# Up projection of a two-layer encoder: all products with rounded weights of a half block ahead of those with remainders, and weight tiles without their offset

## The chip, the core and the metric

The kernel runs on one core of one Trainium2 chip. Its time is device microseconds (us) of one execution, as the median of several runs. Beside the time there is one profiled execution, in which every instruction of every engine has a start and a length.

## What is computed

Two encoder layers over 256 tokens of width 2048, all in float32. Each layer normalises, projects into two groups of attention heads, projects back, normalises again and ends in a gated feed-forward part with a depthwise convolution. The change touches the up projection of that last part, the product `h2 @ w_up[l]` of 256 tokens with 2048 x 11264 weights:

```python
h2 = rms_norm(x, ln2_g[l])
u = depthwise_conv(h2 @ w_up[l], conv_w[l], conv_b[l])
gate, up = u[..., :D_FF], u[..., D_FF:]          # D_FF = 5632
x = x + (jax.nn.silu(gate) * up) @ w_down[l]
```

## The kernel before

A float32 matrix product is made from products of shorter numbers (type float32r). Every operand is split into a rounded part and a remainder. For weights ScalarE writes the rounded part `whi` (line 112) and VectorE the remainder `wlo = raw - whi` (line 113). For tokens the tile `xs[k]` of 128 partitions x 2 x 256 holds the rounded part in slot 0 and the remainder in slot 1, for the k-th of the 16 groups of 128 input columns. Three of the four products of the parts are kept.

All weights come from memory once, in quanta of 128 x 2048 (`raw`, three buffers, issued by the sync engine's queue at line 741). Each quantum is used in two halves of 128 x 1024 (three for some of the down projection). `split_w` (line 751) makes `whi` and `wlo` of a half four halves ahead of its use; there are five buffers of each. A scheduler places the instructions of each engine, with priorities that the code gives; on TensorE the matmuls stand nearly as the code writes them.

The up projection is done in blocks of 128 gate columns and 128 up columns (j = 0 and 1). There are 44 blocks in a layer, 88 in all, each of two quanta, so of four halves; 352 halves in all. One half holds 4 of the 16 k for both j, so 8 weight tiles of 128 x 128. In `q_up` (line 524) the weights are the stationary operand and the tokens move. The helper `two` (line 411) makes two matmuls of a weight tile:

- the rounded weights with both slots of the tokens, 512 columns wide (called a hi product below),
- the remainder with slot 0 of the tokens, 256 columns wide (a lo product).

So one half is hi, lo, hi, lo, ... eight times. When a block's last half is done, `glu` (line 539) reads the sums, applies the convolution and the gate, and splits the result for the down projection.

Everywhere else in the kernel (input, output and down projection) tokens are stationary and 512 weight columns move. The attention of the second head group (`scores` at line 335 and `values` at line 386, through `thrice` at line 328) makes 256-wide float32r matmuls in direct succession.

Where operands lie matters to the change. The tiles of `raw`, `whi`, `wlo`, `mid` and `xs` lie one after the other in each partition's memory, and all their sizes (8192, 4352, 4352, 2048 and 2048 bytes) are whole multiples of 256 bytes, so their starts are equal modulo 256. A weight tile has 1024 + 64 columns of 4 bytes. The up projection uses columns 56 to 1079 of it (`UP_AT = 56`), so its weights start 224 bytes further than its tokens, modulo 256. All other quanta use columns 0 to 1023, in line with what they are multiplied with. "In line" below means: the next weights to be loaded start at the same place modulo 256 bytes as the operand that is moving.

Of the kernel before, what the change touches and what calls it, by code (L numbers as in the profile page):

```python
# [12 lines left out]
F32R = mybir.dt.float32r  # L13
# [5 lines left out]
P = 128  # L19
# [4 lines left out]
KD = D // P  # L24
# [24 lines left out]
SPLIT_AHEAD = 4  # L49
AHEAD_PRIO = 40  # L50
SHIFT = 48

UP_AT = 56
WARM = 14

SPARE = 3 * (("qT", 3),)
# [3 lines left out]
def encoder_kernel(  # L60
# [7 lines left out]
    wp = ctx.enter_context(tc.tile_pool(name="wp", bufs=2))  # L68
# [28 lines left out]
    def mm(ps, lhsT, rhs, start, stop):  # L97
        nc.tensor.matmul(ps, lhsT, rhs, start=start, stop=stop, skip_group_check=True)  # L98
# [10 lines left out]
    def split(hi, lo, src, scale=None):  # L109

        if scale is None:
            high = nc.scalar.activation(hi, src, AF.Copy)  # L112
            nc.vector.tensor_sub(lo, src, hi.bitcast(F32))  # L113
        else:
            high = nc.scalar.activation(hi, src, AF.Copy, scale=scale)  # L115
            nc.vector.scalar_tensor_tensor(lo, src, scale, hi.bitcast(F32),
                                           op0=ALU.mult, op1=ALU.subtract)
        return high
# [7 lines left out]
    xs = {}  # L126
# [281 lines left out]
    def at(q, f, *args, half=1):  # L408
        side.setdefault((q, half), []).append((f, args))

    def two(ps, w_h, w_l, mv, first, last):

        mm(ps, w_h, mv, first, False)
        mm(ps[:, 1], w_l, mv[:, 0], False, last)

    def three(ps, terms, hv, lv, first, last, apart=False):

# [109 lines left out]
    def q_up(l, f, u):  # L527
        def body(q, half, hi, lo):
            if u == 0 and half == 0:
                cur["up"] = psum.tile([P, 2, 2, T], F32, name="mm", bufs=2)  # L530
            ps = cur["up"]
            hv, lv = (w.rearrange("p (k j n) -> p k j n", k=4, j=2) for w in (hi, lo))
            for j in range(2):
                for kk in range(4):
                    k = 8 * u + 4 * half + kk
                    two(ps[:, j], hv[:, kk, j], lv[:, kk, j], xs[k], k == 0, k == KD - 1)
            if u == 1 and half == 1:
                glu(l, f, ps)
        return body

    def glu(l, f, ps):
        ux = halo[f % 2]
        r = T // GRID_W
        t = work.tile([P, 2, T], F32, name="prob", bufs=2)
        nc.scalar.activation(t, ps[:, :, 0], AF.Copy)  # L545
        nc.vector.tensor_add(t, t, ps[:, :, 1])  # L546
        nc.vector.tensor_mul(ux[:, :, r:r + T], t, st["r2"][:, None, :].to_broadcast([P, 2, T]))  # L547

        nc.gpsimd.tensor_copy(ux[:, :, 1:r], ux[:, :, T:T + r - 1])  # L549
        nc.gpsimd.tensor_copy(ux[:, :, T + r:T + 2 * r - 1], ux[:, :, r + 1:2 * r])  # L550
        y = work.tile([P, 2, T], F32, name="pT", bufs=4)
        for j in range(2):
            c = j * NF + f
            w0, w1, w2, b = (par["conv"][:, l, i, c:c + 1] for i in range(4))
            nc.scalar.activation(y[:, j, :], ux[:, j, r:r + T], AF.Identity, scale=w1, bias=b)  # L555
            for w, o in ((w0, 0), (w2, 2 * r)):
                nc.vector.scalar_tensor_tensor(y[:, j, :], ux[:, j, o:o + T], w, y[:, j, :],  # L557
                                               op0=ALU.mult, op1=ALU.add)
        nc.scalar.activation(t[:, 0, :], y[:, 0, :], AF.Silu)  # L559
        m = work.tile([P, T], F32, name="bias", bufs=2)  # L560
        nc.vector.tensor_mul(m, t[:, 0, :], y[:, 1, :])
        gs[f] = middle(l, f)
        split(gs[f][:, 0], gs[f][:, 1], m)
        ms[f] = m
        if f % 2 and f < NF - CHUNKS[-1] + PART:
            sums_mid(l, f // 2, ms.pop(f - 1), ms.pop(f))
# [132 lines left out]
    for l in range(L):  # L699
# [8 lines left out]
        for c, nf in enumerate(CHUNKS):  # L708
            up = lambda f: [(a["w_up"][l, f, u], q_up(l, f, u), "up") for u in range(2)]
# [23 lines left out]
    raw, hl, left, loads, highs = {}, {}, {}, {}, {}  # L733

    def load(q, parts=1):
        if q < len(quanta):
            raw[q] = wp.tile([P, 2048], F32, name="raw", bufs=3)
            left[q] = 3 if quanta[q][2] == "seven" else 2
            m = 2048 // parts
            for j in range(parts):  # L740
                loads[q] = nc.sync.dma_start(out=raw[q][:, j * m:(j + 1) * m], in_=quanta[q][0][:, j * m:(j + 1) * m])

    def split_seven(w, part, hi, lo):

        hv, lv = (t.rearrange("p (k n) -> p k n", k=2) for t in (hi, lo))
        if part == 1:
            nc.vector.tensor_sub(w[:, 1:3], w[:, 1:3], w[:, 2:4])
            nc.vector.tensor_add(w[:, 3], w[:, 3], w[:, 1])
            nc.vector.tensor_sub(w[:, 0], w[:, 3], w[:, 0])
        return split(hv, lv, (w[:, 1::2], w[:, 1:3], w[:, 0::3])[part])  # L750

    def split_w(s, parts=1):
        if s < len(steps):
            q, half = steps[s]
            kind = quanta[q][2]
            o = UP_AT if kind == "up" else 0
            hl[s] = tuple(wp.tile([P, 1024 + 64], F32R, name=t, bufs=SPLIT_AHEAD + 1)[:, o:o + 1024]
                          for t in ("whi", "wlo"))
            with tc.high_priority(offset=AHEAD_PRIO if s >= KD // 2 else 0):
                if kind == "seven":  # L760
                    highs[s] = split_seven(raw[q].rearrange("p (k n) -> p k n", k=4), half, *hl[s])
                else:
                    m = 1024 // parts
                    for j in range(parts):
                        highs[s] = split(*(t[:, j * m:(j + 1) * m] for t in hl[s]),
                                         raw[q][:, half * 1024 + j * m:half * 1024 + (j + 1) * m])
            left[q] -= 1
            if left[q] == 0:
                del raw[q]
                load(q + LOAD_AHEAD)  # L770
# [61 lines left out]
    ps = psum.tile([P, T], F32, name="pv", bufs=1)  # L832
# [3 lines left out]
    for i in range(SPLIT_AHEAD):  # L836
        first_x(i)
        split_w(i, 2 if i == 0 else 1)
# [14 lines left out]
    for s, (q, half) in enumerate(steps):  # L853
        if s + SPLIT_AHEAD < KD // 2:
            first_x(s + SPLIT_AHEAD)
        split_w(s + SPLIT_AHEAD)
        quanta[q][1](q, half, *hl.pop(s))
        for f, args in side.pop((q, half), []):
            f(*args)
# [101 lines left out]
```

## Time and profile before

| what | value |
|---|---|
| median of 3 runs | 2092.17 us (2092.07 to 2092.38) |
| the profiled execution | 2092.0 us, with a span of 2090.2 us from its first to its last instruction |
| TensorE matmuls (PE) busy | 2083.5 us, 100% of the span, 10816 instructions |
| VectorE (DVE) busy | 1720.5 us, 82% |
| ScalarE (ACT) busy | 1222.3 us, 58% |
| GpSimd (POOL) busy | 170.3 us, 8% |
| hi products of the up projection | 2816, mean 390 ns |
| lo products of the up projection | 2816, mean 282 ns |

The matmul's length runs from its start to its modelled end, and the next one starts well before that end; so 390 ns is not the time that a matmul takes from the engine. What it takes is the distance from its start to the start of the next one, called its step below. In the views, L98 is the helper `mm` that issues every matmul; matmuls are told apart by the tiles that they read and write. `PE` rows are matmuls, `PEld` rows the loads of their stationary operand.

### The profile page before, as it was taken

The page shows a single profiled execution, that of the slowest core. Times are in us where ns is not written, and L with a number is a line of the kernel's source. Part 1 is how long each engine was busy: PE and PEld are TensorE (multiplying, and loading weights), DVE is VectorE, ACT ScalarE, POOL GpSimd, SP SyncE. Part 2 cuts the span into 40 slices and gives each one's busy share as a digit, 9 for nine tenths or more (in the row PEclk, how much of TensorE's full clock was granted, in tenths as well). Part 3 has the DMA queues.
Part 4 walks back from the last instruction along what each step waited for, and adds up shares of the span by engine and source line. Part 5 has one row for each costly group of instructions (what it writes and reads, how often), then busy time and mean ns, then how long its engine had stood idle before and what let it go on. Part 6 is the DMA issues. An engine that isn't in the chain of part 4 may idle for free.

```text
span 2090.2 us, 29185 instructions
## 1 busy us (share of the span) xinstructions
PE 2083.5 (100%) x10816; PEld 1789.2 (86%) x10816; DVE 1720.5 (82%) x2604; ACT 1222.3 (58%) x1817; POOL 170.3 (8%) x237
## 2 busy tenths in 40 slices
PE   9999999999999999999999999999999999999999
PEld 8888888888888888888888888888888888888887
DVE  7786757898898988989757866678989989899896
ACT  7566556555555556556555665565556555555563
POOL 0011100100101001010000011001001010010100
PEclk9999999999999999999999999999999999999999
DMA  9544555556565564655655444555555655556554
GB/s 350 199 145 164 179 172 174 198 195 211 180 241 182 208 210 167 242 193 211 208 181 181 162 160 166 177 182 189 214 202 170 236 199 204 201 185 234 185 200 161
DMA packets 62144, 408.42 MB, mean 195 GB/s; under 512 B 7344, under 2 KB 9904, under 8 KB 13744
## 3 DMA queue, kind: packets, MB, share of 16 engines
q1 hardware_dynamic: 61280, 405.46, 56.2%
q8 instruction: 85, 1.39, 0.3%
q10 hardware_dynamic: 720, 1.08, 0.2%
q14 instruction: 59, 0.48, 0.1%
HBM read 404.42 MB, written 2.10 MB: 194 GB/s over the span
## 4 chain that ended last, share of the span: by engine, by line
PE 99%; DMA 0%; ACT 0%; DVE 0%; issue 0%
PE mm L98 90%; PE S L98 4%; PE pv L98 3%; PE tr L98 2%; PE tr L373 1%; PE tr L307 1%; PE S L149 1%; DMA head<-in_head 0%; ACT qtok L274 0%; ACT kT L315 0%; ACT xs L115 0%; DVE x L688 0%; ACT whi L112 0%
## 5 line engine op out<-in xcount | busy, mean ns | idle before, releaser
L112 ACT ACTIVATE whi<-raw 128x1024 fp32r<-128x1024 f32 (+1 forms) x797 | 830.9, 1057 | 689.9 <-PE mm L98 411.9
L113 DVE TENSOR_TENSOR wlo<-raw,whi 128x1024 fp32r<-128x1024 f32 (+1 forms) x797 | 963.9, 1220 | 270.3 <-ACT whi L112 231.8
L98 PE MATMUL mm<-xs,whi 128*128 128x512 f32 x2816 | 977.0, 390 | 0.0
L98 PE MATMUL mm<-xs,wlo 128*128 128x256 f32 x2816 | 794.1, 282 | 0.0
L98 PEld LDWEIGHTS mm<-xs,whi 128*128 128x128 f32 x2816 | 528.3, 188 | 110.5
L98 PEld LDWEIGHTS mm<-xs,wlo 128*128 128x128 f32 x2816 | 532.2, 189 | 1.1
L98 PE MATMUL mm<-whi,mid 128*128 128x512 f32 x1412 | 368.2, 391 | 0.0
L98 PEld LDWEIGHTS mm<-whi,mid 128*128 128x128 f32 x1412 | 263.0, 188 | 53.9
L98 PE MATMUL mm<-whi,xs 128*128 128x512 f32 x1152 | 294.2, 393 | 1.4 <-ACT qtok L274 1.3
L98 PEld LDWEIGHTS mm<-whi,xs 128*128 128x128 f32 x1152 | 213.1, 188 | 44.7 <-ACT qtok L274 1.8
L98 PE MATMUL mm<-wlo,mid 128*128 128x512 f32 x706 | 202.4, 392 | 0.0
L98 PE MATMUL mm<-wlo,xs 128*128 128x512 f32 x576 | 159.5, 393 | 0.0
L98 PEld LDWEIGHTS mm<-wlo,mid 128*128 128x128 f32 x706 | 132.1, 188 | 27.0
L557 DVE SCALAR_TENSOR_TENSOR pT<-halo,conv,pT 128x256 f32<-128x256 f32 x352 | 148.1, 478 | 0.9
L549 POOL COPY halo<-halo 128x6 f32<-128x6 f32 x88 | 39.6, 450 | 1232.6 <-DVE halo L547 1232.6
L98 PEld LDWEIGHTS mm<-wlo,xs 128*128 128x128 f32 x576 | 107.3, 188 | 21.6
L555 ACT ACTIVATE pT<-halo,conv 128x256 f32<-128x256 f32 x176 | 95.1, 587 | 5.8 <-DVE halo L547 5.7
L550 POOL COPY halo<-halo 128x6 f32<-128x6 f32 x88 | 77.1, 876 | 0.2 <-POOL halo L549 0.2
L547 DVE TENSOR_TENSOR halo<-prob,acc_b 128x512 f32<-128x512 f32 x88 | 60.6, 689 | 1.9
L546 DVE TENSOR_TENSOR prob<-prob,mm 128x512 f32<-128x512 f32 x88 | 59.8, 679 | 0.0
L545 ACT ACTIVATE prob<-mm 128x512 f32<-128x512 f32 x88 | 51.3, 583 | 7.1 <-PE mm L98 7.1
L559 ACT ACTIVATE prob<-pT 128x256 f32<-128x256 f32 x88 | 35.5, 404 | 30.0 <-DVE pT L557 30.0
(180 smaller groups left out, 1475.4 us busy)
## 6 DMA issues: line engine op xcount, KB each, us to landing
raw<-in_w_up SPq DMA_DIRECT2D x176, 1024.0 KB, 4.9
raw<-in_w_in SPq DMA_DIRECT2D x71, 1024.0 KB, 4.9
raw<-in_w_down SPq DMA_DIRECT2D x48, 1024.0 KB, 4.8
raw<-in_w_seven SPq DMA_DIRECT2D x40, 1024.0 KB, 4.9
raw<-in_w_out SPq DMA_DIRECT2D x32, 1024.0 KB, 4.9
raw<-in_w_plain SPq DMA_DIRECT2D x10, 1024.0 KB, 4.8
bias<-in_bias SPq DMA_DIRECT2D x16, 160.0 KB, 3.1
x<-in_x SPq DMA_DIRECT2D x4, 512.0 KB, 10.7
```

What stands on the lines that cost most here:

```text
L98: nc.tensor.matmul(ps, lhsT, rhs, start=start, stop=stop, skip_group_check=True)
L112: high = nc.scalar.activation(hi, src, AF.Copy)
L113: nc.vector.tensor_sub(lo, src, hi.bitcast(F32))
L149: nc.tensor.transpose(ps[:, j, tt * P:(tt + 1) * P], x[:, tt, (k + j) * P:(k + j + 1) * P], ident)
L545: nc.scalar.activation(t, ps[:, :, 0], AF.Copy)
L546: nc.vector.tensor_add(t, t, ps[:, :, 1])
L547: nc.vector.tensor_mul(ux[:, :, r:r + T], t, st["r2"][:, None, :].to_broadcast([P, 2, T]))
L549: nc.gpsimd.tensor_copy(ux[:, :, 1:r], ux[:, :, T:T + r - 1])
L550: nc.gpsimd.tensor_copy(ux[:, :, T + r:T + 2 * r - 1], ux[:, :, r + 1:2 * r])
L555: nc.scalar.activation(y[:, j, :], ux[:, j, r:r + T], AF.Identity, scale=w1, bias=b)
L557: nc.vector.scalar_tensor_tensor(y[:, j, :], ux[:, j, o:o + T], w, y[:, j, :], op0=ALU.mult, op1=ALU.add)
L559: nc.scalar.activation(t[:, 0, :], y[:, 0, :], AF.Silu)
```

## The change

The eight hi products of a half come first and then its eight lo products. The constant `UP_AT` and the 64 spare columns of the weight tiles are gone: every weight tile is 128 x 1024, and the up projection's weights start in line with its tokens.

```diff
-
-UP_AT = 56
 WARM = 14
@@
-    def two(ps, w_h, w_l, mv, first, last):
-
-        mm(ps, w_h, mv, first, False)
-        mm(ps[:, 1], w_l, mv[:, 0], False, last)
+    def two(terms):
+
+        for ps, w_h, w_l, mv, first, last in terms:
+            mm(ps, w_h, mv, first, False)
+        for ps, w_h, w_l, mv, first, last in terms:
+            mm(ps[:, 1], w_l, mv[:, 0], False, last)
@@
             hv, lv = (w.rearrange("p (k j n) -> p k j n", k=4, j=2) for w in (hi, lo))
-            for j in range(2):
-                for kk in range(4):
-                    k = 8 * u + 4 * half + kk
-                    two(ps[:, j], hv[:, kk, j], lv[:, kk, j], xs[k], k == 0, k == KD - 1)
+            two([(ps[:, j], hv[:, kk, j], lv[:, kk, j], xs[k], k == 0, k == KD - 1)
+                 for j in range(2) for kk, k in enumerate(range(8 * u + 4 * half, 8 * u + 4 * half + 4))])
@@
-            o = UP_AT if kind == "up" else 0
-            hl[s] = tuple(wp.tile([P, 1024 + 64], F32R, name=t, bufs=SPLIT_AHEAD + 1)[:, o:o + 1024]
-                          for t in ("whi", "wlo"))
+            hl[s] = tuple(wp.tile([P, 1024], F32R, name=t, bufs=SPLIT_AHEAD + 1) for t in ("whi", "wlo"))
```

On TensorE, the second half of a middle block stands like this before (`mm_5708` is the block's accumulator, `xs4_2892` to `xs7_2906` are the tokens of four k, `whi_5610` and `wlo_5611` the half's weights):

```order
L98 MATMUL mm_5708<-xs4_2892,whi_5610 128x512
L98 MATMUL mm_5708<-xs4_2892,wlo_5611 128x256
L98 MATMUL mm_5708<-xs5_2895,whi_5610 128x512
L98 MATMUL mm_5708<-xs5_2895,wlo_5611 128x256
L98 MATMUL mm_5708<-xs6_2903,whi_5610 128x512
L98 MATMUL mm_5708<-xs6_2903,wlo_5611 128x256
L98 MATMUL mm_5708<-xs7_2906,whi_5610 128x512
L98 MATMUL mm_5708<-xs7_2906,wlo_5611 128x256
```

and the same half, on TensorE, with the first two products of the half that follows, stands like this now (the helper is line 96 there):

```order
L96 MATMUL mm_5708<-xs6_2903,whi_5610 128x512
L96 MATMUL mm_5708<-xs7_2906,whi_5610 128x512
L96 MATMUL mm_5708<-xs4_2892,wlo_5611 128x256
L96 MATMUL mm_5708<-xs5_2895,wlo_5611 128x256
L96 MATMUL mm_5708<-xs6_2903,wlo_5611 128x256
L96 MATMUL mm_5708<-xs7_2906,wlo_5611 128x256
L96 MATMUL mm_5708<-xs4_2892,wlo_5611 128x256
L96 MATMUL mm_5708<-xs5_2895,wlo_5611 128x256
L96 MATMUL mm_5708<-xs6_2903,wlo_5611 128x256
L96 MATMUL mm_5708<-xs7_2906,wlo_5611 128x256
L96 MATMUL mm_5708<-xs8_2989,whi_5632 128x512
L96 MATMUL mm_5708<-xs9_2992,whi_5632 128x512
```

The matmuls are the same; runs of eight 512-wide and eight 256-wide ones have taken the place of the alternation, and a run of lo products is followed by the hi products of the next half.

On VectorE, around the end of a layer's first up block, the subtraction of the next weights (`wlo`) and the sum that empties the accumulator (`prob<-prob,mm`) stand like this before:

```order
L113 TENSOR_TENSOR wlo<-raw,whi 128x1024 x3
L546 TENSOR_TENSOR prob<-prob,mm 128x512
L547 TENSOR_TENSOR halo_110<-prob,acc_b 128x2x256
L113 TENSOR_TENSOR wlo<-raw,whi 128x1024
L557 SCALAR_TENSOR_TENSOR pT<-halo_110,conv,pT 128x256 x4
L113 TENSOR_TENSOR wlo<-raw,whi 128x1024
```

and like this now:

```order
L111 TENSOR_TENSOR wlo<-raw,whi 128x1024 x2
L544 TENSOR_TENSOR prob<-prob,mm 128x512
L111 TENSOR_TENSOR wlo<-raw,whi 128x1024
L545 TENSOR_TENSOR halo_110<-prob,acc_b 128x2x256
L111 TENSOR_TENSOR wlo<-raw,whi 128x1024
L555 SCALAR_TENSOR_TENSOR pT<-halo_110,conv,pT 128x256 x4
```

The same instructions stand there; single ones have changed places with a neighbour.

## Rows read from the trace of the kernel before

**Rows 1.** The page: span, busy engines, granted clock, chain that ended last.
```profile
span 2090.2 us, 29185 instructions
PE 2083.5 (100%) x10816; PEld 1789.2 (86%) x10816; DVE 1720.5 (82%) x2604; ACT 1222.3 (58%) x1817; POOL 170.3 (8%) x237
...
PEclk9999999999999999999999999999999999999999
...
PE 99%; DMA 0%; ACT 0%; DVE 0%; issue 0%
PE mm L98 90%; PE S L98 4%; PE pv L98 3%; PE tr L98 2%; PE tr L373 1%; PE tr L307 1%; PE S L149 1%; DMA head<-in_head 0%; ACT qtok L274 0%; ACT kT L315 0%; ACT xs L115 0%; DVE x L688 0%; ACT whi L112 0%
```

**Rows 2.** Waits, TensorE's and ScalarE's: us in total, times, longest us.
```profile
PE mm L98 <- ACT qtok L274: 1.3, 2, 0.7
PE pv L98 <- DVE halfpi L94: 1.1, 1, 1.1
...
ACT whi L112 <- PE mm L98: 411.9, 330, 3.9
```

**Rows 3.** The page's groups, up projection: xcount | busy us, mean ns | idle before.
```profile
L98 PE MATMUL mm<-xs,whi 128*128 128x512 f32 x2816 | 977.0, 390 | 0.0
L98 PE MATMUL mm<-xs,wlo 128*128 128x256 f32 x2816 | 794.1, 282 | 0.0
```

**Rows 4.** Timeline, up projection, TensorE: start us, length us.
```profile
899.45 0.39 PE L98 MATMUL mm<-xs,whi 128*128 128x512 f32 x1
899.67 0.28 PE L98 MATMUL mm<-xs,wlo 128*128 128x256 f32 x1
...
904.99 0.39 PE L98 MATMUL mm<-xs,whi 128*128 128x512 f32 x1
```

**Rows 5.** Timeline, down projection, TensorE: 28 matmuls from first to last row.
```profile
440.28 1.98 PE L98 MATMUL mm<-whi,mid 128*128 128x512 f32 x8
...
446.63 1.52 PE L98 MATMUL mm<-whi,mid 128*128 128x512 f32 x6
```

**Rows 6.** Groups of that stretch, 440.2 to 447.8 us.
```profile
L98 PE MATMUL mm<-whi,mid 128*128 128x512 f32 x18 | 4.7, 389 | 0.0
```

**Rows 7.** Timeline, TensorE, around six 256-wide score matmuls.
```profile
111.22 1.09 PE L98 MATMUL mm<-wlo,xs 128*128 128x512 f32 x4
112.14 0.28 PE L98 MATMUL S<-kTb,qT 128*128 128x256 f32 x1
...
112.86 2.00 PE L98 MATMUL mm<-whi,xs 128*128 128x512 f32 x8
114.70 0.62 PE L98 MATMUL mm<-wlo,xs 128*128 128x512 f32 x2
```

**Rows 8.** Groups, TensorE, 112.15 to 112.90 us (the six score matmuls).
```profile
L98 PE MATMUL S<-mid,qT 128*128 128x256 f32 x2 | 0.6, 283 | 0.0
L98 PE MATMUL S<-kTb,mid 128*128 128x256 f32 x2 | 0.6, 282 | 0.0
L98 PE MATMUL S<-kTb,qT 128*128 128x256 f32 x2 | 0.6, 280 | 0.0
```

**Rows 9.** Groups, TensorE, 112.90 to 114.60 us, then 1153.55 to 1155.5 us.
```profile
L98 PE MATMUL mm<-whi,xs 128*128 128x512 f32 x8 | 2.0, 392 | 0.0
...
L98 PE MATMUL mm<-whi,xs 128*128 128x512 f32 x7 | 1.8, 393 | 0.0
```

**Rows 10.** Timeline, TensorE, after 256-wide matmuls of the values.
```profile
115.84 2.02 PE L98 MATMUL mm<-whi,xs 128*128 128x512 f32 x8
117.69 0.62 PE L98 MATMUL mm<-wlo,xs 128*128 128x512 f32 x2
...
172.07 0.85 PE L98 MATMUL pv<-pT,v_b 128*128 128x256 f32 x6
172.76 1.99 PE L98 MATMUL mm<-whi,xs 128*128 128x512 f32 x8
174.59 0.62 PE L98 MATMUL mm<-wlo,xs 128*128 128x512 f32 x2
```

**Rows 11.** Timeline, TensorE, from the up to the down projection.
```profile
430.75 1.08 PE L98 MATMUL mm<-whi,mid 128*128 128x512 f32 x4
431.67 0.62 PE L98 MATMUL mm<-wlo,mid 128*128 128x512 f32 x2
```

## Prediction

> **What bounds the kernel now.** I read the profile's page first. TensorE is busy for 2083.5 of 2090.2 us, the chain that ended last is 99% TensorE, and the granted clock is at its upper level (2.4 GHz) in all forty slices [rows 1]. The waits come second: TensorE waits for named releasers for 1.3 + 1.1 us in all, and none of these waits is in the up projection, while ScalarE, which makes the rounded weights, waits for TensorE for 411.9 us to get a buffer back [rows 2]. So weights are ready ahead of need, and time can come or go only in the steps of the matmuls.
>
> Third, the groups and the timeline give the steps. The up projection has 2816 hi and 2816 lo products, of mean length 390 and 282 ns [rows 3]. From 899.45 to 904.99 us there are 16 pairs, 5.54 us, so 346 to 347 ns a pair; a hi step is close to 228 ns and a lo step close to 118 (899.67 to the next hi, 346.5 less 228) [rows 4]. A half of eight pairs is 8 x 346.6 = 2.773 us, and 352 halves are 976 us, 47% of the span.
>
> In the down projection, where 512-wide matmuls in line follow each other, 28 of them take 446.63 - 440.28 = 6.35 us: a step of 226.8 ns [rows 5], at a mean length of 389 ns [rows 6]. A hi product is 1 ns longer in length and 1 ns longer in its step than these. A matmul that is held up shows it in its length, nanosecond for nanosecond; that gives steps finer than the 10 ns of the timeline.
>
> **The change part by part.** It adds and removes no matmul, no load and no byte from memory. Three things move.
>
> *The order and the place of the weights* are one term, since they act on the same thing: how long each of the 16 matmuls of a half holds the engine. The trace of before shows what the new sequence is made of, in the attention phase: 512-wide matmuls in line, then six 256-wide score matmuls in line, then 512-wide ones in line [rows 7].
>
> - The lo run. Six 256-wide matmuls take 112.86 - 112.14 = 0.72 us, 120 ns each [rows 7]; their mean lengths, two each of 283, 282 and 280, give 281.7 ns [rows 8], against 282 of the lo products now. Eight such: no gain, no loss, within 1 ns each.
> - The hi run behind it. After the score matmuls the eight 512-wide ones take 114.70 - 112.86 = 1.84 us, not 8 x 226.8 = 1.81 [rows 7]: the first few are held up and the rest fall back to the steady step. Their mean length is 392 ns, and 393 for seven in the same place of the second layer [rows 9], against 390 of the hi products now. That is 2 to 3 ns each, 16 to 24 ns per half; I take 20.
>
> So what the change wins by putting hi products side by side (390 to 389 ns once steady) is less than what it pays at each passage from lo to hi. Before, the alternation had passages too, but their price is already in the 390 and 282. Sum for a half: 8 x 0 + 20 ns; for 352 halves 352 x 20 ns = 7.0 us more.
>
> By the starts alone the sum would be 1.84 + 8 x 0.12 = 2.80 us against 2.773, 27 ns a half or 9.5 us. These starts are rounded to 10 ns, so I stay with the lengths.
>
> Bounds of this term: the cheapest 256-wide run in the trace takes 172.76 - 172.07 = 0.69 us for six, 115 ns each, and the cheapest 512-wide run is the steady one; 8 x 115 + 8 x 226.8 = 2.734 us, 39 ns less than now, 14 us in all. The dearest 512-wide run is 117.69 - 115.84 = 1.85 us; with lo at 120 that is 2.81, 37 ns more, 13 us in all [rows 5, 7, 10]. The score matmuls are nearest in kind, because they alone are in line, as the lo products will be; the values are not.
>
> *The ends of the up projection.* It gives over to the down projection 16 times. Now the four matmuls behind it take 0.92 us where 4 x 226.8 is 0.907 [rows 11], some 10 ns extra; behind a run of lo products I expect the 30 ns (1.84 less 1.81) of rows 7. 16 x 20 ns = 0.3 us.
>
> *Waits.* `whi` is a single tile, needed at the first product of a half as before; `wlo` is now needed 1.8 us into the half instead of 0.2, which only relieves. `whi` is given back some 0.7 us sooner, behind the eighth hi product. VectorE's and ScalarE's instructions change places with neighbours, by a subtraction at a time; ScalarE's 411.9 us of waiting for TensorE [rows 2] is the cover. Cost 0. If that cover failed at every hand-over, the price would be a wait of the size seen, 0.7 us at most [rows 2], in 16 places: 11 us; nothing speaks for it.
>
> *Everything else* keeps its alignment: ten weight tiles shrink by 256 bytes each, so what lies behind them moves by 2560 bytes, a whole multiple of 256. Cost 0: the 18 matmuls of rows 6 take their weights from several of these buffers in turn, and their mean is the steady 389 ns [rows 6].
>
> The Trainium skill speaks against any effect. "TensorE: Matmul & The Clock Gate", Part 2, says that TensorE has two independent SBUF read ports, one for the streaming operand and one for the weight load, so that loading the next weights takes nothing from the running matmul. By that page alone neither address nor order would count and the sum would be 0. The trace disagrees in size: the same 512-wide form has 389 ns in one neighbourhood and 392 to 393 in another [rows 6, 9].
>
> Sum: 2092.0 us of the profiled execution (span 2090.2 and 1.8 around it) + 7.0 + 0.3 = 2099.3 us. That execution lies 0.2 us below the median, which is nothing here.
>
> **The rivals.**
>
> *No change.* The passage from lo to hi costs nothing inside the up projection, because tokens move there and weights are stationary, the other way round than behind the score matmuls. Then a half is 8 x 226.8 + 8 x 120 = 2.774 us, the 2.773 of now: 2092. For it: the alternation has a passage at every pair and still costs only 346.6, which is 226.8 + 120 to a nanosecond [rows 4, 5, 7]. Against: the hold-up comes behind scores and values alike [rows 7, 10]. This is also where that rule of the Trainium skill leads.
>
> *Faster.* The lo run, once by itself, settles in the cheaper state that the six value matmuls reach at 172.07, 115 ns a step, and the hi run behind it costs what it costs there, 174.59 - 172.76 = 1.83 us [rows 10]. A half is 0.92 + 1.83 = 2.75, 23 ns less: 8 us, 2084. It decides as soon as the lo step stays below 117. For it: eight are a longer run than six. Against: those value matmuls are not in line, and the six in line stay at 120.
>
> *Slower still.* The hi run pays what it pays at 115.84, 1.85 us, with lo at 120: 13 us, 2105. Against it: that passage, too, is behind operands out of line.
>
> *The change does not do what it says.* If the weight tiles landed out of line, the price would lie between these; their sizes leave little room.
>
> **How the numbers follow.** My forecast 0.58, no change 0.14, faster 0.15, slower still 0.11, waits or tiles out of place 0.02. About 0.2% (4.2 us) is what a measurement of this kernel tells from no change. Slower by more: 0.58 + 0.11 less a little for a forecast that comes out at half its size, 0.67. Within: 0.17. Faster: 0.16. The forecast's own range is 2096 to 2103 (hi runs at 392 to 393, starts rounded). The range that should hold reaches down through no change, to 2088, and up to 2105.5; it leaves out most of the faster case.
>
> **What would show it.** In the profile after, the group of hi products has a mean of 392 to 393 instead of 390, and lo stays at 281 to 283. In the timeline a half takes 2.79 to 2.80 us, eight hi 1.84 and eight lo 0.95 to 0.96, with the hold-up in the first five hi products. TensorE still waits for next to nothing. A hi mean of 389 or a lo mean below 279 would show the forecast wrong in its first term; new waits of TensorE for `whi` or `wlo` would show the third wrong; other lengths in the down projection the fourth.

## The result, and the profile after

The changed kernel takes 2098.76 us (median of 8 runs, 2098.64 to 2099.07) against 2092.14 us before (8 runs, 2091.98 to 2093.0). The ratio is 1.0031, with a 95% interval of 1.0021 to 1.0041: slower by 6.6 us. The forecast was 2099.3 us, in a range of 2088.0 to 2105.5.

The page of the kernel after gives the span, the busy engines and the two groups of the up projection, with their mean lengths in ns behind the comma. They answer to [rows 1] and [rows 3]:

```profile
span 2097.0 us, 29183 instructions
...
PE 2089.7 (100%) x10816; PEld 1788.5 (85%) x10816; DVE 1722.0 (82%) x2604; ACT 1223.9 (58%) x1817; POOL 108.4 (5%) x237
...
PEclk9999999999999999999999999999999999999999
...
L96 PE MATMUL mm<-xs,whi 128*128 128x512 f32 x2816 | 705.2, 392 | 0.0
...
L96 PE MATMUL mm<-xs,wlo 128*128 128x256 f32 x2816 | 393.5, 282 | 0.0
```

The span grew by 6.8 us, TensorE is still busy all of it at the upper clock, hi products grew from 390 to 392 ns in the mean, and lo products stayed at 282. (The busy time of the groups is a union in time; runs of one kind overlap themselves, so it can't be compared with that of an alternation. The mean can.)

TensorE's waits, in us in total, times, and the longest, answer to [rows 2]:

```profile
PE mm L96 <- ACT qtok L272: 1.3, 2, 0.7
PE pv L96 <- DVE halfpi L92: 1.1, 1, 1.1
PE mm L96 <- ACT whi L110: 0.5, 1, 0.5
```

One wait of 0.5 us is new. It lies ahead of the first product of the input projection, which starts at the same time as before, so it costs nothing (the first row is the kernel before, the second the kernel after; start and length in us):

```profile
6.74 1.26 PE L98 MATMUL mm<-whi,xs 128*128 128x512 f32 x3
6.75 1.25 PE L96 MATMUL mm<-whi,xs 128*128 128x512 f32 x3 [0.46 <-ACT whi L110]
```

So nearly all of the 6.8 us is in the steps of matmuls, where [rows 4] are to be compared with this timeline of the kernel after (start, length of the merged run, count at the end):

```profile
899.04 2.00 PE L96 MATMUL mm<-xs,whi 128*128 128x512 f32 x8
900.89 1.11 PE L96 MATMUL mm<-xs,wlo 128*128 128x256 f32 x8
901.84 2.00 PE L96 MATMUL mm<-xs,whi 128*128 128x512 f32 x8
903.68 1.12 PE L96 MATMUL mm<-xs,wlo 128*128 128x256 f32 x8
904.63 2.00 PE L96 MATMUL mm<-xs,whi 128*128 128x512 f32 x8
```

Eight hi products take 903.68 - 901.84 = 1.84 us, as the eight behind the score matmuls did in [rows 7], eight lo products 0.95, and a half 904.63 - 901.84 = 2.79 us where it was 2.773.

Within one hi run of the kernel after, the groups of the windows 901.9 to 902.95 and 903.05 to 903.6 us show where it is lost: the first five are long in the mean, the last ones nearly steady (the fifth lies in both windows).

```profile
L96 PE MATMUL mm<-xs,whi 128*128 128x512 f32 x5 | 1.3, 394 | 0.0
...
L96 PE MATMUL mm<-xs,whi 128*128 128x512 f32 x4 | 1.1, 390 | 0.0
```

From the start of every matmul in the trace, the mean step at each place of a half can be worked out; here over the halves that stand between two others with nothing else among their products (310 before, 310 after; two more before, behind the mixed products at a layer's first blocks, take 10 ns longer):

```
ns                 hi steps, 1st to 8th                            lo steps, 1st to 8th                        half
before             228.3 each                                      118.3 each                                  2773
after              233.3 235.8 228.3 232.5 230.8 226.7 226.7 226.7 113.3 119.2 120.0 120.0 120.0 120.0 120.0 120.0 2793
```

No place of the half varies by more than 1 ns from one half to the next. The price is not noise that is spread out, but the same sequence 310 times: the hi run takes 14 ns more than before and the lo run 6.

### The profile page after: what moved, and what is told of

Read it like the earlier page. It is cut to its first block, busy times and chain, and to the rows that moved or that the text cites. A ratio compares the mean times of both kernels' runs of the same rounds, so it can differ in the third digit from the quotient of the medians.

```text
span 2097.0 us, 29183 instructions
## 1 busy us (share of the span) xinstructions
PE 2089.7 (100%) x10816; PEld 1788.5 (85%) x10816; DVE 1722.0 (82%) x2604; ACT 1223.9 (58%) x1817; POOL 108.4 (5%) x237
## 4 chain that ended last, share of the span: by engine, by line
PE 99%; DMA 0%; ACT 0%; DVE 0%; issue 0%
PE mm L96 90%; PE S L96 4%; PE pv L96 3%; PE tr L96 2%; PE tr L371 1%; PE tr L305 1%; PE S L147 0%; DMA head<-in_head 0%; ACT qtok L272 0%; ACT kT L313 0%; ACT xs L113 0%; DVE x L686 0%; ACT whi L110 0%
## 5 line engine op out<-in xcount | busy, mean ns | idle before, releaser
L96 PE MATMUL mm<-xs,whi 128*128 128x512 f32 x2816 | 705.2, 392 | 0.0
L96 PEld LDWEIGHTS mm<-xs,whi 128*128 128x128 f32 x2816 | 507.4, 189 | 91.4
L96 PEld LDWEIGHTS mm<-xs,wlo 128*128 128x128 f32 x2816 | 384.2, 190 | 27.3
L96 PE MATMUL mm<-xs,wlo 128*128 128x256 f32 x2816 | 393.5, 282 | 0.0
L547 POOL COPY halo<-halo 128x6 f32<-128x6 f32 x88 | 31.3, 356 | 1301.1 <-DVE halo L545 1301.1
L745 DVE TENSOR_TENSOR raw<-raw 128x1024 f32<-128x1024 f32 x40 | 48.9, 1221 | 0.5
```

## The experiments

"A half" below is the time from the first product of a half block to the first of the next one, read from the starts.

**Order alone, and place alone.** The first has the new order and keeps `UP_AT`, the second keeps the old order with `UP_AT = 0`.

```diff
+            o = 56 if kind == "up" else 0
-            hl[s] = tuple(wp.tile([P, 1024], F32R, ...) ...)
+            hl[s] = tuple(wp.tile([P, 1024 + 64], F32R, ...)[:, o:o + 1024] ...)
```

```diff
-UP_AT = 56
+UP_AT = 0
```

> The new order with the old place of the up projection's weights (224 bytes past the tokens, modulo 256). Theory P (passage): what costs is the passage from a run of 256-wide to a run of 512-wide products, once per half, and it is a matter of the order: hi products at a mean of 392 to 394 ns, the half at 2.79 us, 2098 to 2101 us. Rival A (alignment): the place in line makes the price and the order is free: hi at 389 to 390 ns, 2092 us or up to 3 us less. Rival B (both): out of line a run of 512-wide products is dear at every step (the one such step in the trace of before, behind the up projection's entry, took 235 ns against 227), 8 ns x 8 x 352 = 22 us more, 2114 us.

> The old order (hi, lo, hi, lo) with the weights in line with the tokens. Theory P (passage): every pair has a passage, and in line the first 512-wide step behind a 256-wide one takes 48 of the chip's 2.4 GHz cycles beyond its columns, the 256-wide one behind it 16: 64 together, as before, so 2092 us within 2 us. Rival A (alignment): in line is dearer whatever the order: 20 ns per half more as in the changed kernel, 2098 to 2100 us.

Measured: order alone 2104.06 us, ratio to before 1.0059 (1.0047 to 1.0072); place alone 2110.54 us, 1.0088 (1.0075 to 1.0102). The groups of the order alone, then of the place alone:

```profile
L96 PE MATMUL mm<-xs,whi 128*128 128x512 f32 x2816 | 714.5, 395 | 0.0
...
L96 PE MATMUL mm<-xs,wlo 128*128 128x256 f32 x2816 | 388.5, 280 | 0.0
```

```profile
L98 PE MATMUL mm<-xs,whi 128*128 128x512 f32 x2816 | 995.3, 399 | 0.0
L98 PE MATMUL mm<-xs,wlo 128*128 128x256 f32 x2816 | 790.8, 281 | 0.0
```

With the order alone no hi product of a run comes back to the steady step: their mean step is 233 ns over all eight places, and a half takes 2.800 to 2.809 us. With the place alone the hi products are longest of all, and halves of 2.819, 2.830 and 2.831 us follow each other in turn. So both parts of the change are dearer alone (12 and 18 us) than together (6.6 us): the two effects do not add. Theory P as I had written it falls here. It said that the price belongs to the order, and that the old order in line would cost what it cost before. Rival A, the place alone, falls as well: with the order alone it predicted no price. For the order alone, rival B of its expectation comes nearest: every hi step of a run out of line is dear, by 6.7 ns against the steady 226.7 where it had 8. Its total of 22 us is too large, since the hi step of before is 228.3 and not 227, and the lo steps fall by 0.8 ns.

**Mirrored halves.** Every second half has its lo products first, so that there are runs of 16 and half as many passages from lo to hi.

```diff
-    def two(terms):
+    def two(terms, lo_first=False):
+        n = len(terms)
+        for i in range(2 * n):
+            ps, w_h, w_l, mv, first, last = terms[i % n]
+            if (i < n) != lo_first:
+                mm(ps, w_h, mv, first, last and lo_first)
+            else:
+                mm(ps[:, 1], w_l, mv[:, 0], False, last and not lo_first)
```

> The changed kernel, but every second half block has its lo products first, so that runs of 16 hi and 16 lo products follow each other and there is one passage from lo to hi in two halves. Theory P (passage): the hold-up of 28 ns comes half as often and all else stays at the steady steps (226.7 and 120 ns), so two halves take 5.547 + 0.020 us: 3.5 us less than the changed kernel, 2095 us. Rival A (alignment): every matmul in line pays, whatever its neighbours: no change from the changed kernel, 2098.8 us. Rival C (length): run length itself matters, a longer run drifting into other steps: any step away from 226.7 and 120 ns past the eighth of a run.

Measured: 2106.76 us, ratio 1.0070 (1.0056 to 1.0084), so slower than the changed kernel and not faster. The steps, though, came out as Theory P had them. In the timeline of the mirrored kernel, hi and lo runs of 16:

```profile
898.06 3.82 PE L96 MATMUL mm<-xs,whi 128*128 128x512 f32 x16
901.72 2.08 PE L96 MATMUL mm<-xs,wlo 128*128 128x256 f32 x16
903.63 3.82 PE L96 MATMUL mm<-xs,whi 128*128 128x512 f32 x16
```

Two halves take 903.63 - 898.06 = 5.57 us where 5.567 was expected, and past the eighth product of a run the steps stay at 226.7 and 120 ns, so rival C, the length of a run, is out. By the starts, all up products together take 980.7 us of the span, against 977.1 before and 983.5 in the changed kernel. What ate it is outside: from TensorE's first matmul to the end of its last, everything else takes 1118.3 us here and 1108.2 and 1108.3 there. TensorE's waits of the mirrored kernel hold most of that:

```profile
PE pv L96 <- ACT whi L110: 7.4, 8, 0.9
PE mm L96 <- ACT qtok L272: 1.3, 2, 0.7
PE pv L96 <- DVE halfpi L92: 1.1, 1, 1.1
PE mm L96 <- ACT whi L110: 0.8, 2, 0.6
```

Eight times in the down projection TensorE waits for rounded weights, which it did in neither other kernel. The forecast had priced a wait for weights at up to 0.7 us in each of 16 hand-overs, 11 us, and held it unlikely; here it is 0.9 us in eight places inside the down projection. The last links can be read from the trace around the first of them, at 447.1 us. ScalarE's instruction for those weights starts at 446.02 us, when VectorE's last step on the raw weights (L750) is done. That step starts at 445.22 us, behind another subtraction of 1.22 us. In the changed kernel the down projection begins at nearly the same time (431.4 us against 431.1), and the same step starts at 443.07. ScalarE waits for that step 40 times in the mirrored kernel:

```profile
ACT whi L110 <- DVE raw L750: 38.2, 40, 1.8
```

Why VectorE's instructions stand in another order there was not taken apart.

**The price of each place, under the new order.** One kernel has each of its 88 blocks at another distance between weights and tokens.

```diff
+            o = upno[q] % 64 if kind == "up" else 0    # upno: the block's number, 0 to 87
```

> The changed kernel's order, with the up projection's weights of block n of the 88 at column n modulo 64 of their tiles, so 0 to 252 bytes past the tokens in steps of 4: a look at the price of each place. Theory P (passage): the half takes 2.79 us at nearly all places, and only the size of the hold-up varies. Rival A (alignment): the price falls off with the distance from 0, down to 2.77 us or less over most of the range. If any place lies below 2.76 us (the cheap steps of the value matmuls, 113 to 115 ns, seen for lo), a faster kernel can be made from it.

The time of the whole (2103.59 us, one run) says little here; the halves do. Of a block's four halves the first still carries the state of the block before. Two blocks of this kernel, 28 bytes and then 36 bytes past the tokens, in its timeline:

```profile
1806.15 1.98 PE L96 MATMUL mm<-xs,whi 128*128 128x512 f32 x8
1807.97 1.10 PE L96 MATMUL mm<-xs,wlo 128*128 128x256 f32 x8
1808.90 1.98 PE L96 MATMUL mm<-xs,whi 128*128 128x512 f32 x8
...
1828.46 2.03 PE L96 MATMUL mm<-xs,whi 128*128 128x512 f32 x8
1830.32 1.12 PE L96 MATMUL mm<-xs,wlo 128*128 128x256 f32 x8
1831.28 2.03 PE L96 MATMUL mm<-xs,whi 128*128 128x512 f32 x8
```

Eight bytes between them, and 2.75 us a half against 2.82. Some of the 64 places, with the halves of their blocks in ns, worked out from the starts:

```
bytes past the tokens   halves of the block (of two blocks where two are undivided)
0                       2802 2793 2794 2791
28                      2807 2746 2747 2747 | 2807 2746 2747 2747
32                      2800 2814 2813 2810 | 2801 2813 2813 2810
36                      2763 2827 2827 2823 | 2827 2827 2826 2824
64                      2774 2773 2773 2774 | 2773 2774 2773 2779
156                     2762 2767 2766 2769
192                     2784 2741 2773 2742
224                     2808 2808 2805 2818
```

At 58 of 63 places the median is 2.78 us or more (at the one left, 176 bytes, other work is mixed into the block), so the new order is dear nearly everywhere, as Theory P said, and it does not fall off with the distance as rival A said. But three places, 28, 156 and 192 bytes, are cheaper than the kernel before, and 64 and 120 bytes cost the same. They lie singly: 28 is cheap, 24 and 32 are not.

**Two of the cheap places, by themselves.** The changed kernel with the weights 28 bytes past the tokens, and 192 bytes.

```diff
+            o = 7 if kind == "up" else 0       # and 48 in the other kernel
```

> The changed kernel with the up projection's weights 28 bytes past the tokens (column 7 of their tiles). Theory R: the half takes 2.747 us as in the sweep, 46 ns less than in the changed kernel, 352 halves: 16 us, so 2082 to 2084 us, with hi at 389 ns and lo at 279 ns. Rival S (the sweep's states depend on the block before, which lay elsewhere): the half settles in another state, 2.78 to 2.81 us, 2092 to 2105 us.

> The same with 192 bytes (column 48). In the sweep its halves took 2.742 and 2.773 in turn. Theory R: 2.742 to 2.773 us a half, 2081 to 2092 us. Rival S as before: 2.78 us and more, above 2093 us.

Measured: at 28 bytes 2083.27 us, ratio to before 0.9958 (0.9945 to 0.9972); at 192 bytes 2086.22 us, 0.9973 (0.9962 to 0.9983). Both beat both kernels. The groups and the timeline of the kernel at 28 bytes:

```profile
L96 PE MATMUL mm<-xs,whi 128*128 128x512 f32 x2816 | 696.6, 389 | 0.0
...
L96 PE MATMUL mm<-xs,wlo 128*128 128x256 f32 x2816 | 386.7, 280 | 0.0
```

```profile
900.88 1.98 PE L96 MATMUL mm<-xs,whi 128*128 128x512 f32 x8
902.69 1.10 PE L96 MATMUL mm<-xs,wlo 128*128 128x256 f32 x8
903.63 1.75 PE L96 MATMUL mm<-xs,whi 128*128 128x512 f32 x7
```

A half is 903.63 - 900.88 = 2.75 us. By the starts, hi products stand at the steady 226.7 ns from the second on (227.5 for the first) and lo products at 115 to 117.5: no hold-up behind the passage. From the changed kernel to this one the weights moved by 28 bytes against the tokens, and nothing else moved but by whole multiples of 256 bytes (the 64 spare columns are back): 46 ns a half, 352 halves, 16 us; the medians differ by 15.5. At 192 bytes, halves of 2.741 and 2.773 us alternate, as in the sweep. Rival S, that the sweep's cheap states would not last by themselves, is out for both.

ScalarE and VectorE write the weights at the moved address too, but their writes do not make the price. In the changed kernel two halves pass without ScalarE writing a rounded weight, and three others without VectorE writing a remainder; they take 2793 or 2794 ns like the rest. At 28 bytes such halves take 2747 ns, again like the rest.

**The price of each place, under the old order.** The same sweep with hi and lo alternating.

> The old order (hi, lo, hi, lo), with the weights of block n of the up projection at column n modulo 64 of their tiles: the price of each place under this order. Theory R (relative place): what a half takes is set by how far the weights lie from the tokens modulo 256 bytes together with the order, so under the old order the list of cheap places is another one than under the new: 224 bytes at 2.773 us, 0 at 2.81 to 2.83 us as in the run of the place alone, and the 28 and 192 bytes that are cheap under the new order (2.74 to 2.75 us) not cheap here, or only by chance. Rival A (place alone): the same places are cheap and dear under both orders.

Some of the places (the whole takes 2103.30 us in one run):

```
bytes past the tokens   halves of the block, ns
0                       2773 2773 2774 2775
28                      2817 2827 2826 2822 | 2818 2826 2827 2822
40                      2815 2826 2827 2831 | 2800 2800 2800 2804
192                     2822 2831 2825 2822
224                     2774 2773 2773 2772
```

The list is another one: at 15 of the same 63 places the median is 2.773 or 2.774 us, none has a lower median, and 28 and 192 bytes are among the dear ones. So order and place act together (Theory R), and rival A's one list for both orders is out. Two things did not fit a price that belongs to order and place alone. 0 bytes took 2.773 us here, and 2.82 to 2.83 when all blocks lay at 0. And where two blocks lay at one place they did not always agree: at 40 bytes one has halves of 2815 to 2831 ns, the other of 2800 to 2804.

**Has one place several states?** The old order, first halves of each quantum at 224 bytes, second halves at 0.

```diff
-            o = UP_AT if kind == "up" else 0
+            o = UP_AT if kind == "up" and half == 0 else 0
```

> The old order; of every quantum of the up projection the first half lies 224 bytes past the tokens as before, the second half in line with them. In the sweep of the old order the halves in line took 2.773 us behind a block at 252 bytes, while in the run of the place alone, all in line, they took 2.82 to 2.83. Theory H (history): the same order at the same place has more than one steady state, and which one is taken depends on what ran before; so the halves in line take 2.773 us in one case and 2.82 to 2.83 in another, and here, each behind a half at 224 bytes, all take one of these values, all the same. Rival D (something else in the run of the place alone, such as writes of other engines into the same stretch of memory, made it dear): the halves in line scatter between 2.77 and 2.83 us.

Measured: 2100.97 us in one run. Of the halves at 224 bytes nearly all take 2.774 to 2.777 us; of the halves in line 170 take 2.818 to 2.820. Two take 2.774; these stand behind the mixed products at a layer's first blocks. Groups of two neighbouring halves of this kernel, in line first:

```profile
L98 PE MATMUL mm<-xs,whi 128*128 128x512 f32 x8 | 2.9, 398 | 0.0
```

```profile
L98 PE MATMUL mm<-xs,whi 128*128 128x512 f32 x8 | 2.8, 390 | 0.0
```

All but two at one value, with no scatter, and not the one of the sweep: Theory H holds and rival D is out. The same order at the same place has at least two steady states, 2.773 and 2.82 us a half. So "place alone costs 18 us" is true of that kernel and not of the place.

That what ran before picks the state can be seen inside one kernel, the one of the order alone, where place and order are the same for all halves. Each layer's first stretch of the up projection begins with blocks whose products are mixed with each other and with other work, and then 28 halves in a row take 2.800 us. All other stretches begin behind the down projection, and there halves of 2.805 and 2.808 us alternate, to a nanosecond. Two starts from the first stretch and two from a later one:

```profile
400.96 2.03 PE L96 MATMUL mm<-xs,whi 128*128 128x512 f32 x8
...
403.76 2.03 PE L96 MATMUL mm<-xs,whi 128*128 128x512 f32 x8
```

```profile
901.08 2.03 PE L96 MATMUL mm<-xs,whi 128*128 128x512 f32 x8
...
903.89 2.03 PE L96 MATMUL mm<-xs,whi 128*128 128x512 f32 x8
```

Which part of what ran before counts, no run shows.

**All tiles moved together.** `SHIFT = 48` to `SHIFT = 20` moves weights and tokens by the same 96 bytes (a tile of 48 columns takes 192 bytes of a partition, and one of 20 columns takes 96).

> The changed kernel with all tiles behind the first one moved by 96 bytes, weights and tokens together, so that their distance stays 0. Theory R: only the distance counts, so a half of the up projection takes 2.793 us as in the changed kernel. Rival B (place of each by itself, in banks of the memory): the half takes another time. The other phases may change through tiles that did not move (the residual x).

Measured: 2098.59 us in one run. Halves take 2793 and 2794 ns, with the same step at each of the 16 places to the nanosecond, so it is the distance that counts and not where weights or tokens lie by themselves. Rival B of this expectation (each place by itself) is out.

**All other quanta at other places.** The kernel at 28 bytes, with the 512-wide matmuls of all other phases at column n modulo 64.

```diff
+            o = 7 if kind == "up" else other[q] % 64   # other: the quantum's number among the rest
```

> The changed kernel's order with the up projection at 28 bytes, and the weights of all other quanta (512-wide, moving, with tokens stationary) at column n modulo 64 of their tiles, n counting these quanta. Theory R (relative place): a run of 512-wide products alone has a step that depends on the place: 226.7 ns in line, 233 to 235 ns at most places, and perhaps below 226 at a few. Rival A: 226.7 ns is a floor for them at any place. If some place lies below 225 ns, the down projection can be made faster in the same way.

Measured: 2110.53 us in one run. The two largest groups of matmuls outside the up projection, in the kernel before and then here:

```profile
L98 PE MATMUL mm<-whi,mid 128*128 128x512 f32 x1412 | 368.2, 391 | 0.0
L98 PE MATMUL mm<-whi,xs 128*128 128x512 f32 x1152 | 294.2, 393 | 1.4 <-ACT qtok L274 1.3
```

```profile
L96 PE MATMUL mm<-whi,mid 128*128 128x512 f32 x1412 | 376.5, 397 | 0.0
L96 PE MATMUL mm<-whi,xs 128*128 128x512 f32 x1152 | 300.3, 398 | 1.3 <-ACT qtok L272 1.3
```

Here the tokens are loaded and the weights move. Sorted by the distance (how far the tokens start past the weights, modulo 256 bytes), the median step is 227 ns at 0, 16 and 144 bytes and 229 to 240 at all others; none is below 226. So the step depends on the place, as Theory R said, but for pure 512-wide runs rival A is right that the steady step in line is the floor: no place of this sweep is cheaper.

## Why the prediction was right

*The lo run.* Forecast: no gain, no loss, 282 ns. Measured 282 ns in the mean. By the starts it is 6 ns a half dearer (952 ns against 947), a size that the lengths in whole ns did not show.

*The hi run.* Forecast: eight in 1.84 us, mean 392 to 393 ns, the first five held up. Measured 1.84 us, 392 ns, and steps above the steady one at the first five places. Against the hi products of before that is 14 ns a half (against a steady run it is 27), less than the 16 to 24 ns that the forecast read from lengths in whole ns. With the 6 ns of the lo run it makes the 20 ns that the sum used. So the total was right and its split was not: that the two errors cancel is luck.

*The sum.* 352 halves by 20 ns were to be 7.0 us, and 0.3 us for the 16 ends of the up projection. By the starts the up products take 6.5 us more, everything else up to the end of the last matmul 0.1 us more, and what follows that 0.2 us more. The passage out of the up projection costs what was forecast: the first eight matmuls of the down projection behind it take 1841 ns where they took 1822, so 19 ns more in 16 places, 0.3 us. But the term of the ends left out that the first half of each of these 16 stretches now has no passage in front. In the kernel after, behind the down projection:

```profile
472.20 1.98 PE L96 MATMUL mm<-xs,whi 128*128 128x512 f32 x8
474.01 1.12 PE L96 MATMUL mm<-xs,wlo 128*128 128x256 f32 x8
474.97 2.00 PE L96 MATMUL mm<-xs,whi 128*128 128x512 f32 x8
```

That half takes 2.77 us, and its hi run 1.81. 16 x 27 ns = 0.4 us less takes back the 0.3 us and a little more.

*Waits and the rest.* Forecast 0; the one new wait of 0.5 us moves nothing, and all other phases together differ by 0.1 us, the 0.3 us behind the passages included.

*What carried the forecast* is that the trace of before held the new sequence in small: 512-wide in line, 256-wide in line, 512-wide in line, in the attention phase [rows 7]. With both the order and the place equal, its steps could be taken over whole. Read to the nanosecond, the six score matmuls there have steps of 113, 119 and four times 120 ns, and the eight behind them 234, 235, 229, 232, 231, 227, 226 and 227: the sequence of the kernel after, place by place. Carried on to eight lo products that is 2793 ns a half, and 20 ns more, from the trace of before alone. The reason I gave to it afterwards, that the passage has a price that belongs to the order, is only half of it. The same order costs 2.75 us a half at 28 bytes, with no hold-up behind the passage, and 2.80 at 224. Had the change been one of its halves alone, the same reasoning would have said 2098 to 2101 and 2092 us, and the runs say 2104 and 2111.

*The rule of the Trainium skill* ("TensorE: Matmul & The Clock Gate", Part 2: two independent SBUF read ports, so that loading the next weights takes nothing from the running matmul) led to the rival of no change. The measurements decide against that rival, and against the step that led to it, that neither address nor order would count: 28 bytes of address move a half by 46 ns. Whether it is these two reads that collide, no run shows.

*Open* is what collides with what. Distance, order and the state left by what ran before decide the step, and a hold-up lengthens the matmul itself (hi products of 394 ns at the start of a run and 390 at its end). That the reading of the moving operand and the load of the next weights get in each other's way in the memory fits all of this, but no run took the load away, so it stays an argument.

## What to carry to other kernels

Where TensorE is busy for the whole span, look for a place in the trace where the new sequence already runs, with the same widths and the same relative addresses, and take over its steps, the transient behind each change of width included; do not argue from one of the two alone. The distance between stationary and moving operands modulo 256 bytes is worth a sweep whenever the order changes, since the best place of one order is a bad one of the other; one kernel that gives every block another distance shows all of them in a single profile. Then run the chosen place by itself, since a sweep's block inherits its state from its neighbour.

## What was not expected of the hardware

The same matmuls in the same order at the same distance have more than one steady state (2.773 and 2.82 us a half), chosen by what ran before; in the kernel of the order alone the states are 2.800 us, and 2.805 with 2.808 in turn. And one group off the critical path moved a lot: the second halo copy on GpSimd took 876 ns in the mean before and takes 266 after, here in the kernel after:

```profile
L548 POOL COPY halo<-halo 128x6 f32<-128x6 f32 x88 | 23.4, 266 | 0.2 <-POOL halo L547 0.2
```

It took 289 ns with the place alone, 824 ns in the fastest kernel, and 899 ns with the places reset (2101 us), so it goes with neither the order nor the time of the whole. The traces show why. A copy takes either 0.2 us or more than 0.9. Each of the 57 long ones of the kernel before starts up to 0.3 us behind the start of a VectorE subtraction of weights (1.2 us) and ends 0.05 us behind its end; the kernel after has seven such copies. The short ones start where no such subtraction runs, with its start, or within 0.02 us of its end. One pair from the kernel before:

```profile
908.67 1.26 POOL L550 COPY halo<-halo 128x6 f32<-128x6 f32 x1
...
908.65 1.23 DVE L113 TENSOR_TENSOR wlo<-raw,whi 128x1024 fp32r<-128x1024 f32 x1 [0.24 <-ACT whi L112]
```

So the mean tells in how many blocks the copy falls just behind the start of such a subtraction.
